# Second FFN, gate and up: seven block products in place of eight for the first four k tiles

## The chip, the cores and the metric

One core of a Trainium2 chip runs the whole kernel. The engines are TensorE (PE; its weight loads are listed apart as PEld), VectorE (DVE), ScalarE (ACT), GpSimd (POOL) and SyncE (SP), which issues most of the DMAs. Every engine takes its instructions in the order of its own queue and waits on semaphores for the others. The metric is the device time in microseconds of one execution, a median over runs; the profile is of one execution.

## The reference

One layer of a streaming encoder on 256 rows (two row tiles of 128) and D = 2048 columns, all in f32. What matters here are the two half-FFNs, one ahead of the mixer and one behind it:

```
x = x + 0.5 * swiglu(rms_norm(x, ffn2_norm), ffn2_w_gate, ffn2_w_up, ffn2_w_down)
swiglu(h, w_gate, w_up, w_down) = (silu(h @ w_gate) * (h @ w_up)) @ w_down
```

w_gate and w_up are 2048 x 5632, w_down is 5632 x 2048. Ahead of the second FFN come the mixer (a state space model and an attention) and its output projection, behind it a gate with a per-layer embedding.

## The kernel before

**Precision.** Each f32 operand is split into two fp32r parts: hi is the rounded copy (ScalarE, L168), lo the rest (VectorE, L171). A product is three matmuls: hi by hi, activation lo by weight hi, activation hi by weight lo. The activation is the stationary operand (128 x 128), the weight the moving one (128 x 512).

**Tiles.** K = 2048 is 16 k tiles of 128. The FFN's columns are 11 blocks (f = 0 to 10) of 512. A raw weight load brings four k tiles of one block, 1 MB, into one of three `raw` buffers (L282). It is split in two halves of two k tiles each; a half's hi and lo (`whi`, `wlo`, four buffers each) are called a weight tile here. `gemm_half` runs one weight tile: two k tiles by two row tiles by three matmuls, 12 in all, the eight that read hi first and the four that read lo last (L292, L293, L297). `gemm_block` does this for the 16 k tiles of one matrix: eight weight tiles.

**The FFN.** For each column block `ffn` runs gate, then up, 16 weight tiles in all. ScalarE turns the gate's sum into silu (L440), VectorE multiplies it with up's sum out of PSUM (L464). Two weight tiles later VectorE transposes the result in 32-blocks into `mid` (L203, `turn_blocks`), and for every pair of blocks 16 DMAs a further eight weight tiles later write the turned activation for the down product (L216). Block 0 of the second FFN instead runs gate and up in turns (`gemm_pair`), because the last quarters of its input come late.

**Order.** `step()` is called after each weight tile and advances whatever was put off. A scheduler then orders the instructions of each engine ahead of time, so what stands in a queue is fixed in the built program. PSUM has four one-bank tiles (`acc`) and two two-bank tiles (`aux`). `sg`, the gate's tile, has one buffer, `h` two. Normalised input: the gain is in the activation parts, the row factor r (`xn.rs`) is applied at the end, to both sums.

Lines of the kernel before that the steps touch: the split 168 and 171, the raw load 282, the matmuls 292, 293 and 297, the silu 440, the final product 464, the transposes 203 and the turning DMAs 216. These lines lie ahead of the change and keep their numbers in the changed kernel, but for 440 and 464, which become 555 and 580 and serve block 0 alone in the second FFN.

Of the kernel before, what the change touches and what calls it, by code (L numbers as in the profile page):

```python
# [9 lines left out]
F32 = mybir.dt.float32  # L10
F32R = mybir.dt.float32r
I32 = mybir.dt.int32
AF = mybir.ActivationFunctionType
ALU = mybir.AluOpType
AX = mybir.AxisListType

P = 128
# [9 lines left out]
NB = 512  # L27
# [6 lines left out]
def layer_kernel(ctx: ExitStack, tc: tile.TileContext, a: dict, shapes: dict, out: bass.AP):  # L34
    nc = tc.nc
# [8 lines left out]
    TT = T // P  # L44
    ND = D // NB
    KD = D // P
# [7 lines left out]
    wp = ctx.enter_context(tc.tile_pool(name="wts", bufs=4))  # L54
# [9 lines left out]
    def uid(s):  # L64
        count[0] += 1
        return f"{s}_{count[0]}"

    def get(pool, tag, width=1024, bufs=1):
        return pool.tile([P, width], F32, tag=tag, name=uid(tag), bufs=bufs)

    def com(tag):
        return get(comp, tag, *{"sg": (1024, 1), "h": (1024, 2), "sq": (NB, 1), "mid": (2048, 1)}[tag])

    def phase(name):
        return tc.tile_pool(name=name, bufs=1, reuse_waits="tile")

    def aux(s="aux"):
        return auxp.tile([P, 1024], F32, tag="aux", name=uid(s))

    def acc(s="acc"):  # L80
        return accp.tile([P, NB], F32, tag="acc", name=uid(s))
# [4 lines left out]
    def halves(kind):  # L86

        return [
            actp.tile([P, 4, T], F32R, tag=kind + s, name=uid(kind + s), bufs={"n": 4, "h": 2}[kind])
            for s in ("hi", "lo")  # L90
        ]
# [4 lines left out]
    def start(g):  # L96
        beside.append(g)
        return g

    def step():  # L100
        for g in list(beside):
            if next(g, beside) is beside:
                beside.remove(g)

    def finish(g):
        for _ in g:
            pass

    def put_off(steps, fn, *args):


        def g():
            for _ in range(steps):
                yield
            fn(*args)

        return start(g())

    def pin(ins):
        return tc.keep_in_program_order(ins)  # L120
# [44 lines left out]
    def split(hi, lo, src, scale=None, pinned=False):  # L165

        if scale is None:
            copy = nc.scalar.copy(hi, src)  # L168
            if pinned:
                pin(copy)  # L170
            nc.vector.tensor_tensor(out=lo, in0=src, in1=hi.bitcast(F32), op=ALU.subtract)  # L171
        else:
            split_each(hi.unsqueeze(1), lo.unsqueeze(1), src.unsqueeze(1), [scale])
# [50 lines left out]
    def by_tile(out, nk):  # L224

        return out.rearrange("p (x f b) -> p f x b", f=nk, b=32)
# [51 lines left out]
    def weight_halves(w, k0, nk, n0, own=None):  # L278

        raw = wp.tile([P, 4, NB], F32, tag="raw", name=uid("raw"), bufs=3)  # L280
        src = w[k0 * P : (k0 + nk) * P, n0 : n0 + NB].rearrange("(j p) n -> p j n", p=P)
        nc.sync.dma_start(raw[:, :nk, :], src)  # L282
        return weight_split(raw, nk, own)

    def gemm_half(ps, half, ts, start, stop, cols=slice(0, NB)):

        (ahi, alo), (h, hi, lo) = half
        for j in range(2):
            for t in ts:
                lh = ahi[:, 2 * h + j, t * P : (t + 1) * P]  # L290
                ll = alo[:, 2 * h + j, t * P : (t + 1) * P]
                nc.tensor.matmul(ps[t], lhsT=lh, rhs=hi[:, j, cols], start=start and j == 0, stop=False)  # L292
                nc.tensor.matmul(ps[t], lhsT=ll, rhs=hi[:, j, cols], start=False, stop=False)  # L293
        for j in range(2):
            for t in ts:
                lh = ahi[:, 2 * h + j, t * P : (t + 1) * P]
                nc.tensor.matmul(ps[t], lhsT=lh, rhs=lo[:, j, cols], start=False, stop=stop and j == 1)  # L297
# [46 lines left out]
    class Normed:  # L344
# [61 lines left out]
        def rs(self, t):  # L406
            return self.r[:, t : t + 1]

    def ffn(i, xn, nxt, bg=None):
        wg, wu, wd = (a[f"ffn{i}_w_{s}"][0] for s in ("gate", "up", "down"))  # L410
        hT = []
        pools = ExitStack()
        early = 8 if bg else NF
        hp = pools.enter_context(phase(f"h{i}"))
        side = ExitStack()
        prep = bg(side) if bg else None
        mids = {}

        def turned(hp, f, hh):
            pair, n_pair = f // 2, min(2, NF - f // 2 * 2) * 4  # L420
            if f % 2 == 0:
                mids[pair] = com("mid")[:, : 128 * TT * n_pair].rearrange(
                    "p (q t f b) -> p q t f b", q=4, t=TT, b=32
                )
            for t in range(TT):
                turn_blocks(mids[pair], hh[:, t * NB : (t + 1) * NB], t, f % 2 * 4, 4)
            if f % 2 or f == NF - 1:
                hf = get(hp, f"hT{pair}", T * n_pair)
                turn_quarters(hf, mids[pair], 8)
                hT.append(by_tile(hf, n_pair))  # L430

        for f in range(NF):
            if prep and f == min(early, NF - 1):
                finish(prep)
                side.close()
                prep = None
                hp = pools.enter_context(phase(f"h{i}b"))
            def gate():
                for t in range(TT):
                    nc.scalar.activation(sg[:, t * NB : (t + 1) * NB], pg[t], AF.Silu, scale=xn.rs(t))  # L440

            first = ()
            if f == 0 and bg:
                warm_up(10)
                first = first_quarters(wg, xn)
            if f == 0 and not bg:
                both = gemm_pair(xn, ((wg, 0), (wu, 0)), KD)
                pg = next(both)
            else:
                pg = gemm_block(xn, wg, f * NB, KD, first)  # L450
            sg = com("sg")
            if f == 0 and bg:
                for n in range(ND):
                    put_off(n, load_x, n)
                    put_off(n + 2, xn.squares, n)
                put_off(6, gate)
            else:
                gate()
            pu = gemm_block(xn, wu, f * NB, KD) if f or bg else next(both)
            if prep and f == 0:  # L460
                start(prep)
            hh = com("h")
            for t in range(TT):
                nc.vector.scalar_tensor_tensor(  # L464
                    out=hh[:, t * NB : (t + 1) * NB], in0=pu[t], scalar=xn.rs(t),
                    in1=sg[:, t * NB : (t + 1) * NB], op0=ALU.mult, op1=ALU.mult,
                )
            put_off(2, turned, hp, f, hh)

        def act(k):  # L470
            hi, lo = halves("h")
            split(in_32(hi), in_32(lo), hT[k // 2][:, k % 2 * 4 : k % 2 * 4 + 4])
            return hi, lo

        for n in range(ND):
            ps = gemm_block(act, wd, n * NB, F // P)
            for t in range(TT):
                nc.vector.scalar_tensor_tensor(
                    out=xt[t][n], in0=ps[t], scalar=0.5, in1=xt[t][n], op0=ALU.mult, op1=ALU.add
                )  # L480
            put_off(0 if n == ND - 1 and n < nxt.early else 2, nxt.block, n)
        pools.close()
# [701 lines left out]
    q0, k0, v0 = SW, SW + NH * DH, SW + 2 * NH * DH  # L1184
    mix, s5p, atp = ExitStack(), ExitStack(), ExitStack()
    mixp = mix.enter_context(phase("mix"))
    pool = s5p.enter_context(phase("s5"))
# [10 lines left out]
    pool = atp.enter_context(phase("attn"))  # L1198
# [19 lines left out]
    both = gemm_pair(lambda k: yss[k], [(sides[0], n * NB) for n in range(2)], SW // P)  # L1218
    for n, side in ((0, 0), (1, 0), (0, 1), (1, 1), (2, 0), (2, 1), (3, 0), (3, 1)):
        y, r = ((yss, rss), (ysb, rsb))[side]  # L1220
        ps = next(both) if n < 2 and not side else gemm_block(lambda k: y[k], sides[side], n * NB, SW // P)
        for t in range(TT):
            nc.vector.scalar_tensor_tensor(
                out=xt[t][n], in0=ps[t], scalar=r[0][:, t : t + 1], in1=xt[t][n], op0=ALU.mult, op1=ALU.add
# [47 lines left out]
    wg = a["w_ple_gate"][0]  # L1272
# [4 lines left out]
    n = ND - 1  # L1277
# [4 lines left out]
    def add(t, n_, r):  # L1282
        x, g = xt[t][n_], es[n_][:, t * NB : (t + 1) * NB]
        nc.vector.scalar_tensor_tensor(out=x, in0=g, scalar=r, in1=x, op0=ALU.mult, op1=ALU.add)
        nc.sync.dma_start(out[0, t * P : (t + 1) * P, n_ * NB : (n_ + 1) * NB], x)

    t = 0
    sigmoid(gate, t, next(gates))
    ple(n, t, gate, next(projs))
    s = small(1)  # L1290
# [7 lines left out]
    t = 1  # L1298
# [3 lines left out]
    early, part, ms, root, r, tmp = (small(1) for _ in range(6))  # L1302
# [9 lines left out]
    for c, (ahead, total) in enumerate(((early, part), (part, ms))):  # L1312
# [3 lines left out]
            out=com("sq")[:, :W], in0=gate[:, cols[c]], scalar=1.0, in1=gate[:, cols[c]], op0=ALU.mult, op1=ALU.mult,  # L1316
# [9 lines left out]
    both = aux()  # L1326
    pin(nc.tensor.matmul(both[:, :NB], lhsT=ident, rhs=xt[t][by_pe], start=True, stop=False, skip_group_check=True))
    for _ in range(10):
# [4 lines left out]
    both = both[:, :NB]  # L1333
# [7 lines left out]
        both, lhsT=diag, rhs=es[by_pe][:, t * NB : (t + 1) * NB], start=False, stop=True, skip_group_check=True  # L1341
# [93 lines left out]
```

## Time and profile before

| what | us |
|---|---|
| median of three runs | 1879.47 (1879.34 to 1879.84) |
| span of the profiled execution | 1878.1 |
| TensorE busy | 1869.5 |
| VectorE busy | 1184.8 |
| ScalarE busy | 963.8 |

The page gives the span of the profiled execution, from the first to the last instruction; it has no separate total time, so the span stands in for it, 1.4 us under the median of the runs. In the views, "x" is a count, "mean ns" the duration of one instruction, and what stands in brackets is the idle time ahead of it on its engine, with what ended it. "us to landing" of a DMA counts from its issue. Matmul durations overlap, since they are pipelined; their spacing is the cost. VectorE's and ScalarE's durations overlap by a little too.

### The profile page before, as it was taken

To read this page: it belongs to the slowest core of one execution; us is meant where nothing else is said; L and a number is where in the kernel's file an instruction comes from. 1 tells how busy PE (TensorE), PEld (TensorE's weight loads), DVE (VectorE), ACT (ScalarE), POOL (GpSimd) and SP (SyncE) were. 2 spreads that over 40 slices of the span, in tenths; PEclk is the share of its full clock that TensorE was granted. 3 is DMA by queue.
4 is the path that set the end of the run, shared out by engine and by line. 5 is a ranking of instruction groups with operands and counts; after the bars stand their busy time and mean duration, and the time that the engine had idled before them with its cause. 6 is when DMAs were issued, how large, how long until landed. Compare 5 with 4: busy or idle time off the path is not lost.

```text
span 1878.1 us, 23877 instructions
## 1 busy us (share of the span) xinstructions
PE 1869.5 (100%) x9194; PEld 1549.5 (83%) x9194; DVE 1184.8 (63%) x1391; ACT 963.8 (51%) x1110; POOL 50.3 (3%) x84
## 2 busy tenths in 40 slices
PE   9999999999999999999999999999999999999998
PEld 7888888888888888888888888888888888888887
DVE  8867665444676776696566655455545566777655
ACT  7444444444455665455785544444444455666554
POOL 0011000000000000010020000000000000000000
PEclk9999999999999999999999999999999999999999
DMA  8788867766665667675646657666667665666563
GB/s 320 246 274 269 265 209 228 225 211 212 207 204 201 197 212 234 186 263 155 217 136 223 222 186 220 195 209 201 205 201 220 191 222 195 203 211 205 181 235 124
DMA packets 230387, 400.07 MB, mean 213 GB/s; under 512 B 26401, under 2 KB 50337, under 8 KB 229985
## 3 DMA queue, kind: packets, MB, share of 16 engines
q1 hardware_dynamic: 227824, 392.81, 65.2%
q0 software_dynamic: 1728, 4.33, 0.7%
q8 instruction: 72, 1.18, 0.3%
q10 hardware_dynamic: 720, 1.41, 0.2%
q14 instruction: 43, 0.34, 0.1%
HBM read 369.26 MB, written 9.83 MB: 202 GB/s over the span
## 4 chain that ended last, share of the span: by engine, by line
PE 97%; ACT 2%; DMA 0%; POOL 0%; issue 0%; SPq 0%; POOLq 0%
PE acc L292 32%; PE acc L297 32%; PE acc L293 32%; PE aux L899 0%; ACT whi L168 0%; DMA raw<-in_ffn_w_gate 0%; ACT nhi L178 0%; POOL sqg L1090 0%; PE aux L843 0%; PE aux L982 0%; PE aux L716 0%; ACT sg L1161 0%; PE aux L1015 0%; ACT L1161 0%; ACT L1034 0%
## 5 line engine op out<-in xcount | busy, mean ns | idle before, releaser
L171 DVE TENSOR_TENSOR wlo<-raw,whi 128x1024 fp32r<-128x1024 f32 x666 | 811.8, 1225 | 587.0 <-ACT whi L168 579.1
L168 ACT CAST whi<-raw 128x1024 fp32r<-128x1024 f32 x666 | 699.5, 1055 | 835.0 <-PE acc L293 776.2
L292 PE MATMUL acc<-whi,nhi 128*128 128x512 f32 x1568 | 613.5, 391 | 0.8 <-ACT whi L168 0.4
L293 PE MATMUL acc<-whi,nlo 128*128 128x512 f32 x1568 | 610.5, 389 | 0.0
L297 PE MATMUL acc<-wlo,nhi 128*128 128x512 f32 x1568 | 420.7, 389 | 0.0
L292 PE MATMUL acc<-whi,hhi 128*128 128x512 f32 x1056 | 410.8, 389 | 0.0
L293 PE MATMUL acc<-whi,hlo 128*128 128x512 f32 x1056 | 410.8, 389 | 0.0
L292 PEld LDWEIGHTS acc<-whi,nhi 128*128 128x128 f32 x1568 | 294.5, 188 | 63.9 <-ACT whi L260 1.3
L297 PEld LDWEIGHTS acc<-wlo,nhi 128*128 128x128 f32 x1568 | 294.3, 188 | 61.7 <-DVE wlo L171 0.4
L293 PEld LDWEIGHTS acc<-whi,nlo 128*128 128x128 f32 x1568 | 294.6, 188 | 60.3
L297 PE MATMUL acc<-wlo,hhi 128*128 128x512 f32 x1056 | 282.2, 389 | 0.0
L293 PEld LDWEIGHTS acc<-whi,hlo 128*128 128x128 f32 x1056 | 198.3, 188 | 41.2
L297 PEld LDWEIGHTS acc<-wlo,hhi 128*128 128x128 f32 x1056 | 198.2, 188 | 41.1
L292 PEld LDWEIGHTS acc<-whi,hhi 128*128 128x128 f32 x1056 | 198.2, 188 | 41.1
L171 DVE TENSOR_TENSOR hlo<-hT,hhi 128x1024 fp32r<-128x1024 f32 x88 | 107.2, 1219 | 0.0
L168 ACT CAST hhi<-hT 128x1024 fp32r<-128x1024 f32 x88 | 91.6, 1042 | 0.1
L464 DVE SCALAR_TENSOR_TENSOR h<-acc,sm,sg 128x512 f32<-128x512 f32 x44 | 31.0, 747 | 23.7 <-PE acc L297 23.7
L440 ACT ACTIVATE sg<-acc,sm 128x512 f32<-128x512 f32 x44 | 27.7, 681 | 6.8 <-PE acc L297 5.1
L203 DVE STREAM_TRANSPOSE mid<-h 128x512 f32<-128x512 f32 x44 | 28.6, 689 | 0.0
L829 POOL COPY dec<-rho 128x512 f32<-128x512 f32 x8 | 9.6, 1233 | 540.9 <-DVE hlo L171 441.6
L1322 POOL TENSOR_SCALAR sm<-sm,sm 128x1 f32<-128x1 f32 x1 | 0.3, 258 | 881.1 <-DVE sq L1315 881.1
L180 DVE SCALAR_TENSOR_TENSOR nlo<-h,gains,nhi 128x256 fp32r<-128x256 f32 x52 | 22.8, 489 | 1.2 <-ACT nhi L178 1.2
(251 smaller groups left out, 657.5 us busy)
## 6 DMA issues: line engine op xcount, KB each, us to landing
raw<-in_ffn_w_up SPq DMA_DIRECT2D x88, 1024.0 KB, 5.7
raw<-in_ffn_w_down SPq DMA_DIRECT2D x88, 1024.0 KB, 5.1
raw<-in_ffn_w_gate SPq DMA_DIRECT2D x86, 1024.0 KB, 5.2
raw<-in_w_in SPq DMA_DIRECT2D x32, 1024.0 KB, 5.7
raw<-in_w_out SPq DMA_DIRECT2D x16, 1024.0 KB, 5.3
raw<-in_w_ple_gate SPq DMA_DIRECT2D x16, 1024.0 KB, 5.4
hT<-mid SPq DMA_DIRECT2D x160, 64.0 KB, 4.9
h<-mid SPq DMA_DIRECT2D x176, 32.0 KB, 3.7
```

The source lines that it names most:

```text
L168: copy = nc.scalar.copy(hi, src)
L171: nc.vector.tensor_tensor(out=lo, in0=src, in1=hi.bitcast(F32), op=ALU.subtract)
L180: nc.vector.scalar_tensor_tensor(out=lo[:, j], in0=src[:, j], scalar=scale, in1=hi[:, j].bitcast(F32), op0=ALU.mult, op1=ALU.subtract,)
L203: nc.vector.transpose(mid[:, :, t, k0 : k0 + nk, :].rearrange("p q f b -> p f q b"), src.rearrange("p (f q b) -> p f q b", f=nk, q=4),)
L292: nc.tensor.matmul(ps[t], lhsT=lh, rhs=hi[:, j, cols], start=start and j == 0, stop=False)
L293: nc.tensor.matmul(ps[t], lhsT=ll, rhs=hi[:, j, cols], start=False, stop=False)
L297: nc.tensor.matmul(ps[t], lhsT=lh, rhs=lo[:, j, cols], start=False, stop=stop and j == 1)
L440: nc.scalar.activation(sg[:, t * NB : (t + 1) * NB], pg[t], AF.Silu, scale=xn.rs(t))
L464: nc.vector.scalar_tensor_tensor(out=hh[:, t * NB : (t + 1) * NB], in0=pu[t], scalar=xn.rs(t), in1=sg[:, t * NB : (t + 1) * NB], op0=ALU.m ...
L829: nc.gpsimd.tensor_copy(dvw[:, e], rho4[:, r0 : r0 + 4].unsqueeze(1).unsqueeze(3).to_broadcast([P, 2, 4, NC]))
L1322: pin(nc.gpsimd.tensor_scalar(total, square, 1.0 / D, ahead, op0=ALU.mult, op1=ALU.add))
```

## The change

In blocks 1 to 10 of the second FFN the first four k tiles of gate and up are computed together. Take the activation's four k tiles as a 2 x 2 block matrix A (rows: row tiles 0 and 1; columns: k tiles 0 and 1, and 2 and 3), and the weights as B (rows: k tiles 0 and 1, and 2 and 3; columns: gate and up; b11 and b21 are gate's halves, b12 and b22 up's). The four output blocks are a product of two 2 x 2 block matrices, which takes eight block products of two k tiles each; here it takes seven, with summed rows of A and summed columns of B:

- weight sums on VectorE (L459): t1 = b11 + b12, t2 = t1 + b22, t4 = t2 + b21, t3 = b12 + b22, two buffers; each is split into hi and lo like a weight (`shi`, `slo`, three buffers). Signs are put into the row sums.
- row sums once, in block 0 (`sum_forms`, L412 to L426), split into hi and lo.
- products in the order b11, b21, t1, t2, t4, t3, b22 (`product`, L452, L453, L455), six matmuls each, with both raw tiles held until all sums are made.
- the products of b21 and t4 stay open in PSUM and take the gate's other 12 k tiles, that of b22 and the bank beside it take up's. After the first four steps the row tiles are done one after the other in each weight tile.
- what the sums share is added at the end: L531 copies the first product out of PSUM (ScalarE), L532 and L533 add the products of t2 and t3 to it, L537 adds the gate's two sums and L538 is the silu, L540 subtracts from the product of t1 (both row tiles at once), L545 adds up's sums, L547 is the final product.

```diff
@@ -406,11 +406,99 @@
         def rs(self, t):
             return self.r[:, t : t + 1]
 
+    def sum_forms(parts):
+
+        hi, lo = parts
+        whole, sums = com("h"), com("h")
+        u = whole.rearrange("p (j t m) -> p j t m", j=4, t=TT)
+        nc.vector.tensor_tensor(
+            out=whole.rearrange("p (j t) -> p j t", j=4), in0=hi.bitcast(F32), in1=lo.bitcast(F32), op=ALU.add
+        )
+        s = sums.rearrange("p (z j m) -> p z j m", z=4, j=2)
+        up, down = u[:, :2], u[:, 2:]
+        for z, (x, y, op) in enumerate((
+            (up[:, :, 1], down[:, :, 1], ALU.subtract), (s[:, 0], up[:, :, 0], ALU.subtract),
+            (up[:, :, 0], up[:, :, 1], ALU.subtract), (down[:, :, 0], s[:, 1], ALU.add),
+        )):
+            nc.vector.tensor_tensor(out=s[:, z], in0=x, in1=y, op=op)
+        both = halves("n")
+        split(*both, sums.rearrange("p (z t) -> p z t", z=4))
+        return both
+
+    def gemm_seven(act, sums, ws, n0, nkt, pool, first, second):
+
+        raws = []
+        for w in ws:
+            raw = wp.tile([P, 4, NB], F32, tag="raw", name=uid("raw"), bufs=3)
+            nc.sync.dma_start(raw, w[: 4 * P, n0 : n0 + NB].rearrange("(j p) n -> p j n", p=P))
+            raws.append(raw)
+        b11, b21, b12, b22 = (raw[:, 2 * h : 2 * h + 2, :] for raw in raws for h in range(2))
+        parts = act(0)
+
+        def whole(k, t):
+            return [[u[:, 2 * k + j, t * P : (t + 1) * P] for j in range(2)] for u in parts]
+
+        def summed(z):
+            return [[u[:, z, j * P : (j + 1) * P] for j in range(2)] for u in sums]
+
+        def product(ps, left, src, own, stop):
+            hi, lo = (
+                (pool if own else wp).tile([P, 2, NB], F32R, tag=s, name=uid(s), bufs=3 if own else None)
+                for s in (("shi", "slo") if own else ("whi", "wlo"))
+            )
+            split(hi, lo, src)
+            lh, ll = left
+            for j in range(2):
+                nc.tensor.matmul(ps, lhsT=lh[j], rhs=hi[:, j], start=j == 0, stop=False)
+                nc.tensor.matmul(ps, lhsT=ll[j], rhs=hi[:, j], start=False, stop=False)
+            for j in range(2):
+                nc.tensor.matmul(ps, lhsT=lh[j], rhs=lo[:, j], start=False, stop=stop and j == 1)
+
+        def add(x, y):
+            t = pool.tile([P, 2, NB], F32, tag="sum", name=uid("sum"), bufs=2)
+            nc.vector.tensor_tensor(out=t, in0=x, in1=y, op=ALU.add)
+            return t
+
+        p1, p2 = acc(), acc()
+        product(p1, whole(0, 0), b11, False, True)
+        product(p2, whole(1, 0), b21, False, False)
+        step()
+        t1 = add(b11, b12)
+        p5 = acc()
+        product(p5, summed(0), t1, True, True)
+        t2 = add(t1, b22)
+        p67 = aux()
+        product(p67[:, :NB], summed(1), t2, True, True)
+        step()
+        t4 = add(t2, b21)
+        p4 = acc()
+        product(p4, whole(1, 1), t4, True, False)
+        t3 = add(b12, b22)
+        product(p67[:, NB:], summed(2), t3, True, True)
+        step()
+        p38 = aux()
+        product(p38[:, :NB], summed(3), b22, False, False)
+        step()
+        put_off(0, first, p1, p67)
+        for w, banks, fresh in ((ws[0], [p2, p4], False), (ws[1], [p38[:, :NB], p38[:, NB:]], True)):
+            for k0 in range(4, nkt, 4):
+                part = act(k0 // 4)
+                for half in list(weight_halves(w, k0, 4, n0)):
+                    begin = k0 == 4 and half[0] == 0
+                    end = k0 + 4 >= nkt and half[0] == 1
+                    for t in range(TT):
+                        gemm_half({t: banks[t]}, (part, half), (t,), fresh and t == 1 and begin, end)
+                    step()
+            if not fresh:
+                put_off(0, second, p2, p4, p5)
+        return p38
+
     def ffn(i, xn, nxt, bg=None):
         wg, wu, wd = (a[f"ffn{i}_w_{s}"][0] for s in ("gate", "up", "down"))
         hT = []
         pools = ExitStack()
         early = 8 if bg else NF
+        sevens = None if bg else pools.enter_context(phase(f"sums{i}"))
         hp = pools.enter_context(phase(f"h{i}"))
         side = ExitStack()
         prep = bg(side) if bg else None
@@ -435,6 +523,33 @@
                 side.close()
                 prep = None
                 hp = pools.enter_context(phase(f"h{i}b"))
+            if sevens and f:
+                sg, hh = com("sg"), com("h")
+                gate_cols, up_cols = ([u[:, t * NB : (t + 1) * NB] for t in range(TT)] for u in (sg, hh))
+
+                def opened(p1, p67, g=gate_cols, u=up_cols):
+                    nc.scalar.copy(g[0], p1)
+                    nc.vector.tensor_tensor(out=u[0], in0=p67[:, :NB], in1=g[0], op=ALU.add)
+                    nc.vector.tensor_tensor(out=u[1], in0=p67[:, NB:], in1=u[0], op=ALU.add)
+
+                def gated(p2, p4, p5, g=gate_cols, u=up_cols, hh=hh):
+                    for z, (ps, other) in enumerate(((p2, g[0]), (p4, u[1]))):
+                        nc.vector.tensor_tensor(out=g[z], in0=ps, in1=other, op=ALU.add)
+                        nc.scalar.activation(g[z], g[z], AF.Silu, scale=xn.rs(z))
+                    v = hh.rearrange("p (t n) -> p t n", t=TT)
+                    nc.vector.tensor_tensor(
+                        out=v, in0=p5.unsqueeze(1).to_broadcast([P, TT, NB]), in1=v, op=ALU.subtract
+                    )
+
+                p38 = gemm_seven(xn, sums, (wg, wu), f * NB, KD, sevens, opened, gated)
+                nc.vector.tensor_tensor(out=hh, in0=p38, in1=hh, op=ALU.add)
+                for t in range(TT):
+                    nc.vector.scalar_tensor_tensor(
+                        out=up_cols[t], in0=up_cols[t], scalar=xn.rs(t), in1=gate_cols[t], op0=ALU.mult, op1=ALU.mult
+                    )
+                put_off(2, turned, hp, f, hh)
+                continue
+
             def gate():
                 for t in range(TT):
                     nc.scalar.activation(sg[:, t * NB : (t + 1) * NB], pg[t], AF.Silu, scale=xn.rs(t))
@@ -446,6 +561,7 @@
             if f == 0 and not bg:
                 both = gemm_pair(xn, ((wg, 0), (wu, 0)), KD)
                 pg = next(both)
+                sums = sum_forms(xn(0))
             else:
                 pg = gemm_block(xn, wg, f * NB, KD, first)
             sg = com("sg")
```

## The prediction

> **What bounds the kernel now.** I read the first part of the page, the clock, the shares of the chain that ended last, and then one column block of the second FFN's gate and up in the stage view and in order of time.
>
> ```profile
> span 1878.1 us, 23877 instructions
> PE 1869.5 (100%) x9194; PEld 1549.5 (83%) x9194; DVE 1184.8 (63%) x1391; ACT 963.8 (51%) x1110; POOL 50.3 (3%) x84
> ...
> PEclk9999999999999999999999999999999999999999
> ...
> PE 97%; ACT 2%; DMA 0%; POOL 0%; issue 0%; SPq 0%; POOLq 0%
> ```
>
> TensorE runs all the time at the full clock and is the chain. A matmul taken away is therefore time taken away, and a wait put in front of a matmul is time added. The next fence is the stage view of one whole block (columns: TensorE, its loads, VectorE, ScalarE, GpSimd, clock, DMA share, GB/s), then the end of one block and the start of the next in order of time.
>
> ```profile
> 1182.68:1226.20 43.52, 43.52 (x193) 36.04 (x192) 22.02 (x21) 18.07 (x19) 0.00 (x0) 1.00 0.61 194
> ```
>
> ```profile
> 1179.96 0.39 PE L292 MATMUL acc<-whi,nhi 128*128 128x512 f32 x1
> ...
> 1180.35 1.23 DVE L171 TENSOR_TENSOR wlo<-raw,whi 128x1024 fp32r<-128x1024 f32 x1 [1.50 <-ACT whi L168]
> ...
> 1181.98 1.06 ACT L168 CAST whi<-raw 128x1024 fp32r<-128x1024 f32 x1 [1.66 <-PE acc L293]
> 1182.66 1.41 DVE L464 SCALAR_TENSOR_TENSOR h<-acc,sm,sg 128x512 f32<-128x512 f32 x2 [1.09 <-PE acc L297]
> 1182.68 0.39 PE L292 MATMUL acc<-whi,hhi 128*128 128x512 f32 x1
> ...
> 1183.98 1.22 DVE L171 TENSOR_TENSOR wlo<-raw,whi 128x1024 fp32r<-128x1024 f32 x1
> ...
> 1185.12 1.30 DVE L203 STREAM_TRANSPOSE mid<-h 128x512 f32<-128x512 f32 x2
> 1185.23 0.37 SPq L282 DMA_DIRECT2D raw<-in_ffn_w_up  x1
> 1185.40 0.39 PE L292 MATMUL acc<-whi,hhi 128*128 128x512 f32 x1
> ```
>
> A weight tile (two k tiles, 12 matmuls) takes 1182.68 to 1185.40, 2.72 us, or 0.2267 us a matmul; 192 of them are the 43.52 us. ScalarE's cast starts 2.02 us into a tile, when the hi matmuls have let go of a buffer: it fills the tile four ahead. So TensorE has three tiles, 8 us, in hand, and VectorE idles 1.5 us per tile. Back to back VectorE's spacing is less than the duration: two L464 take 1.32 us (1182.66 to 1183.98), a split 1.14 (to 1185.12). The raw load is issued 0.03 us after the split that frees its buffer (1185.20).
>
> **The change, part by part.**
>
> *Matmuls.* In ten of eleven blocks the first four k tiles took 48 matmuls and take 42. 60 x 0.2267 = 13.6 us less, if nothing waits. Six matmuls in a row now go to one bank; the last block of the final gate (per-layer embedding) already does that, and its pace is the same:
>
> ```profile
> 1846.82 0.39 PE L292 MATMUL acc<-whi,nhi 128*128 128x512 f32 x1
> ...
> 1848.19 0.39 PE L292 MATMUL acc<-whi,nhi 128*128 128x512 f32 x1
> ```
>
> Six in 1.37 us. So this edit costs nothing of itself.
>
> *VectorE and ScalarE on average.* The prices (groups with shapes: of the block ending at 1182.68, then of the whole span):
>
> ```profile
> L171 DVE TENSOR_TENSOR wlo<-raw,whi 128x1024 fp32r<-128x1024 f32 x16 | 19.6, 1222 | 20.4 <-ACT whi L168 18.9 <-DMA hT<-mid 1.5
> L168 ACT CAST whi<-raw 128x1024 fp32r<-128x1024 f32 x17 | 18.0, 1057 | 27.1 <-PE acc L293 27.1
> L203 DVE STREAM_TRANSPOSE mid<-h 128x512 f32<-128x512 f32 x2 | 1.3, 690 | 0.0
> L440 ACT ACTIVATE sg<-acc,sm 128x512 f32<-128x512 f32 x2 | 1.3, 680 | 0.0
> ```
>
> ```profile
> L725 DVE TENSOR_TENSOR t<-bt,coef 128x1024 f32<-128x1024 f32 x8 | 9.7, 1221 | 0.1
> L860 DVE TENSOR_TENSOR rt<-aux,rot 128x1024 f32<-128x1024 f32 x4 | 4.9, 1222 | 6.1 <-PE aux L843 6.1
> L1284 DVE SCALAR_TENSOR_TENSOR x<-e,sm,x 128x512 f32<-128x512 f32 x7 | 4.8, 748 | 0.1
> L1252 DVE TENSOR_TENSOR h<-acc,h 128x512 f32<-128x512 f32 x7 | 4.5, 684 | 7.3 <-PE acc L297 7.3
> ```
>
> Seven splits for four: +3 x 1.222. Four weight sums (priced as L725): 4 x 1.221. Four 512-wide adds from PSUM (L532, L533, two L537; as L1252): 4 x 0.684. L540 and L545 (as L860): 2 x 1.222. The two final products stay at 0.748. Together 13.7 us, so VectorE goes from 22.0 to 35.7 us in a block of 42.2; ScalarE from 18.1 by three casts and a copy to 21.9. Neither becomes the bound on average. But nearly all of it falls around the 9.5 us of the seven products, where a buffer feeds 6 matmuls (1.36 us) instead of 12 (2.72), and that stretch must be walked.
>
> *The order.* Both engines run in the built program's order, which has two forms. Form A (blocks 1, 2, 4, 6, 8, 10; block 1 with the old finish), VectorE: sums t1, t2; splits b11, t1, b21, t2; sum t4; split b22; L545 of the block before; split t4; its two L547; sum t3; its two transposes; split of the next gate tile, R1; split t3. Form B (3, 5, 7, 9): splits b11, b21; t1, t2; splits t1, b22; L545; split t2; two L547; t4; a transpose; t3; split t4; a transpose; split t3.
>
> *When it can start.* Let the first product start at 0, so the twelfth tile R12 starts at -2.72 and R7 at -16.32. t1 needs both raw tiles; up's is loaded into the buffer that the split of R10 frees. That split stands behind the two L537, and the second of these waits for R6's last matmul: -16.1 to -15.4. The split ends at -14.2, the load is issued and lands 5.6 us later (limits 5.0 and 6.4), at -8.6:
>
> ```profile
> raw<-in_ffn_w_up SPq DMA_DIRECT2D x40, 1024.0 KB, 5.6
> raw<-in_ffn_w_gate SPq DMA_DIRECT2D x37, 1024.0 KB, 5.2
> ```
>
> ```profile
> DMA to landing us min/median/max: 5.0/5.6/6.4
> ```
>
> VectorE is then free (R12's split, whose cast waits for R8's hi matmuls, ends at -8.8).
>
> *Form A.* From -8.6: t1 1.25 (t2 needs its result, so its full duration), eleven more of 1024 columns at the spacing 1.14, two L547 1.32, two transposes 1.22 (0.61 each: the 1.30 for two less the last one's 0.69). That is 16.3 us: the split of t3 starts at 7.7 and ends at 9.0. TensorE reaches that product, the sixth, at 5 x 1.36 = 6.8. Its hi part is cast at 7.1 (on ScalarE it stands behind the cast of R3, whose load follows t4 and lands 5.2 us on), and its lo part is wanted at 8.0. Wait 0.3 + 1.0 = 1.3 us.
>
> *Form B.* The split of b21 comes first, and its cast waits for R10's hi matmuls (-5.7): cast to -4.6, split to -3.4. Only then t1 (1.25), t2 (1.3, since the next split waits for t1's cast) and four spacings of 1.14, which bring L547 to 3.7; t4 ends at 6.3, its cast at 7.35; t3 ends at 8.0, split t4 at 9.2, split t3 at 10.9. TensorE wants t4's hi at 5.44 (1.9 late), its lo 0.9 later than it then comes to it, t3's lo 0.4 later. Wait 3.2 us.
>
> Block 1 has no L545 ahead of the chain: 0.2. Sum of the waits: 0.2 + 5 x 1.3 + 4 x 3.2 = 19.5 us. What is late next recovers: R2's split is 3 us early in either form, and each later tile gives back 1.5.
>
> *Other edits.* The forms of the summed rows (L414 to L427) add four 256-wide adds and two 1024-wide instructions to VectorE, about 4 us, in block 0, whose VectorE idles half the time:
>
> ```profile
> 1080.00:1090.00 10.00, 10.00 (x46) 8.28 (x45) 4.61 (x4) 3.67 (x4) 0.00 (x0) 1.00 0.58 185
> ```
>
> Zero; without the cover at most those 4 us. DMA: the same loads and bytes. L433 on SP's queue holds back nothing needed sooner: in form B the second gate load follows t4 and lands at 11.5, and R3 is due at 18. L537 on VectorE holds R10's split, counted above. The other PSUM readers wait for groups already closed.
>
> *Sum.* -13.6 + 19.5 = +5.9 us. On the profiled span 1878.1 that is 1884.0; the runs' median 1879.47 lies 1.4 above the span, so 1885.4, taken as 1885.5. The ends of the waits: load landing in 5.0 us gives form A 1.0 and 17.9 in all (1883.8); every spacing at the row's full 1.22 instead of 1.14 gives 2.2 and 3.8, 26.4 in all (1892.3), and a landing at 6.4 besides some 0.8 more per form A (1896). I take 1.14, because it is measured between just such neighbours. A shorter spacing than 1.14 is not in the rows, but the sums are no splits: at 1.05 the waits would be 12.9, level with the saving.
>
> [...]
>
> **Rivals.** *Faster (the waits stay under the saving).* One mechanism: the queue from the up load's landing to the split of t3 is shorter than walked, since TensorE's three tiles in hand, or tighter spacing of the sums, cover it. It decides at a mean wait of 1.36 us per block, a queue about 0.7 us shorter in both forms. For it: VectorE's 1.5 us idle per tile; against: the lead is one of buffers that hold half as much work here. With no wait at all, 1879.5 - 13.6 = 1865.9. *No change.* The same queue 0.2 to 1 us shorter: 1876 to 1883. *Longer.* Full durations and late landings together: 1896 and above. *The clock.* If TensorE's waits, up to 1.9 us each, made it run the next tile at half speed, each block would lose another 2.7 us: 1912. Every row here has 1.00, but none has such waits. [...] That the change removes fewer matmuls than said is excluded: the built order has the six per block gone.
>
> **How the numbers follow.** What a measurement can tell from no change is 0.2%, 3.8 us. The forecast, slower by 4 to 17 us, has 0.66; longer 0.05 and the clock 0.02; no change 0.17; faster 0.10. The range 1880 to 1897 takes in the ends above and the upper part of no change. Slower 0.73, same 0.17, faster 0.10.
>
> **What would show it.** Right: 60 matmuls fewer; TensorE idle in every block at L452 or L455, on VectorE's split or ScalarE's cast of a sum, about 1.3 us in even blocks and 3 us in odd ones from 3 on; blocks of 43.5 and 45.4 us in turn (42.16 plus the wait). Wrong: blocks of 42.2 us with no idle (the lead covers), waits at the first or second product (loads late), or at R1 to R4 (VectorE not recovering), or a granted clock under 1.

## The result and the profile after

The changed kernel takes 1871.32 us (median of four runs, 1870.86 to 1872.24) where the kernel before, measured beside it, takes 1879.65 us. The ratio is 0.9954, with a 95% interval of 0.9940 to 0.9968: it is faster by 8.3 us; the ratio gives 0.46%. The forecast was 1885.5 us with a range of 1880 to 1897, and slower as the likeliest case. It was wrong in sign.

The page of the changed kernel, its first part, its clock row and the shares of the chain that ended last:

```profile
span 1870.4 us, 23938 instructions
...
PE 1859.4 (99%) x9134; PEld 1536.3 (82%) x9134; DVE 1310.4 (70%) x1527; ACT 996.5 (53%) x1151; POOL 50.4 (3%) x84
...
PEclk9999999999999999999999999999999999999999
...
PE 92%; ACT 3%; DVE 2%; DMA 1%; SPq 1%; issue 1%; POOL 0%; DVEq 0%; ACTq 0%; POOLq 0%
```

The 60 matmuls are gone (9194 to 9134), VectorE has 125.6 us more work, and TensorE is still busy 99% of the span. The stage view of two blocks in a row (columns: length, then busy time and count of TensorE, its loads, VectorE, ScalarE and GpSimd, then clock, DMA share and GB/s):

```profile
1139.79:1182.26 42.47, 42.47 (x187) 34.83 (x186) 31.14 (x31) 20.55 (x22) 0.00 (x0) 1.00 0.71 223
1182.26:1225.14 42.88, 42.74 (x187) 34.68 (x186) 37.31 (x37) 22.09 (x24) 0.00 (x0) 1.00 0.57 196
```

A block of 186 matmuls without a wait would be 186 x 0.2267 = 42.17 us; before it was 43.52. So block 2 loses 0.3 us to waits and block 3 0.7, where 1.3 and 3.2 were forecast. The even blocks that follow lose 0.2 each and the odd ones 0.7 to 0.8. Over the ten blocks the waits come to 4.1 us (block 1 has 0.1), not 19.5. The groups of TensorE's waits in the ten blocks (its loads' rows, in total, times, longest) show the same:

```profile
PEld aux L452 <- ACT shi L168: 2.7, 5, 0.6
PEld aux L455 <- DVE slo L171: 1.0, 4, 0.2
PEld acc L452 <- ACT shi L168: 0.9, 4, 0.2
PEld acc L297 <- DVE wlo L171: 0.9, 4, 0.2
```

A load's row counts time in which the matmuls before it still run (at 1191.36, in block 3, the row has 0.57 us, and the matmul before ends at 1191.22, 0.14 us ahead), so the rows don't add up to the 4.1 us. The first three stand where the waits were forecast, at the products of the sums, on the cast or split of a sum; the fourth, 0.2 us a time, is an ordinary weight tile. Only the size is a fifth. What makes them short is seen in the order of time. First block 2 (form A), from its first matmul; TensorE and VectorE only:

```profile
1139.79 0.39 PE L452 MATMUL acc<-whi,hhi 128*128 128x512 f32 x1
...
1146.73 0.50 PE L452 MATMUL aux<-shi,nhi 128*128 128x512 f32 x1
...
1147.20 1.21 DVE L171 TENSOR_TENSOR slo<-sum,shi 128x1024 fp32r<-128x1024 f32 x1
...
1147.76 0.40 PE L452 MATMUL aux<-whi,nhi 128*128 128x512 f32 x1
...
1148.70 0.62 PE L455 MATMUL aux<-slo,nhi 128*128 128x512 f32 x2
...
1149.16 0.63 PE L455 MATMUL aux<-wlo,nhi 128*128 128x512 f32 x2
```

VectorE makes t3's lo from 7.41 to 8.62 us into the block, much as walked (7.7 to 9.0). But TensorE does not ask for it at 8.0. The matmuls of the seventh product, b22's (`aux<-whi`, L452), stand in its queue between t3's hi and t3's lo. The lo is wanted at 8.91 us, and it is there. Then block 3 (form B):

```profile
1187.75 0.40 PE L452 MATMUL aux<-whi,nhi 128*128 128x512 f32 x1
...
1188.68 0.62 PE L455 MATMUL aux<-wlo,nhi 128*128 128x512 f32 x2
...
1189.14 0.40 PE L292 MATMUL acc<-whi,hhi 128*128 128x512 f32 x1
...
1189.60 0.46 PE L452 MATMUL acc<-shi,hhi 128*128 128x512 f32 x1
...
1190.07 1.22 DVE L171 TENSOR_TENSOR slo<-sum,shi 128x1024 fp32r<-128x1024 f32 x1
...
1190.59 0.40 PE L292 MATMUL acc<-whi,hhi 128*128 128x512 f32 x1
...
1191.36 0.50 PE L452 MATMUL aux<-shi,nhi 128*128 128x512 f32 x1
...
1191.70 0.63 PE L455 MATMUL acc<-slo,hhi 128*128 128x512 f32 x2
1191.83 1.19 DVE L171 TENSOR_TENSOR slo<-sum,shi 128x1024 fp32r<-128x1024 f32 x1
...
1193.54 0.63 PE L455 MATMUL aux<-slo,nhi 128*128 128x512 f32 x2
```

Here the whole product of b22 (1187.75 to 1189.14) and two matmuls of the next gate tile R1 (L292, line 292 being the ordinary weight tiles) run before t4's product starts at 1189.60, and more of R1's matmuls stand between t4's hi and lo and between t3's hi and lo. t4's hi is taken at 7.34 us into the block instead of 5.44, t3's lo at 11.28, when VectorE has had it ready since 10.76 (walked 10.9).

The sum against the spans: -13.6 + 4.1 = -9.5, measured 1870.4 - 1878.1 = -7.7. The other 1.8 us lie ahead of the change: block 1 starts 1.9 us later than before. Most of that is one row of the waits ahead of it:

```profile
PE aux L959 <- issue: 1.4, 1, 1.4
```

L959 is a matmul of the state-space stage that the change does not touch; whether this belongs to the change is tested below.

### The profile page after: what moved, and what is told of

It is laid out like the page before. It is cut to its first block, busy times and chain, and to the rows that moved or that the text cites. A ratio compares the mean times of both kernels' runs of the same rounds, so it can differ in the third digit from the quotient of the medians.

```text
span 1870.4 us, 23938 instructions
## 1 busy us (share of the span) xinstructions
PE 1859.4 (99%) x9134; PEld 1536.3 (82%) x9134; DVE 1310.4 (70%) x1527; ACT 996.5 (53%) x1151; POOL 50.4 (3%) x84
## 4 chain that ended last, share of the span: by engine, by line
PE 92%; ACT 3%; DVE 2%; DMA 1%; SPq 1%; issue 1%; POOL 0%; DVEq 0%; ACTq 0%; POOLq 0%
PE acc L292 26%; PE acc L297 26%; PE acc L293 26%; PE aux L293 3%; PE aux L292 3%; PE aux L297 3%; ACT whi L168 1%; SPq L1061 1%; PE acc L455 1%; DMA raw<-in_w_in 1%; PE aux L452 1%; PE acc L452 1%; PE acc L453 1%; PE aux L455 1%; PE aux L453 1%
## 5 line engine op out<-in xcount | busy, mean ns | idle before, releaser
L171 DVE TENSOR_TENSOR wlo<-raw,whi 128x1024 fp32r<-128x1024 f32 x656 | 798.2, 1224 | 458.9 <-ACT whi L168 455.3
L292 PE MATMUL acc<-whi,nhi 128*128 128x512 f32 x1408 | 551.0, 391 | 1.2 <-ACT whi L260 0.5
L293 PE MATMUL acc<-whi,nlo 128*128 128x512 f32 x1408 | 548.2, 389 | 0.0
L292 PE MATMUL acc<-whi,hhi 128*128 128x512 f32 x816 | 317.6, 389 | 0.0
L293 PE MATMUL acc<-whi,hlo 128*128 128x512 f32 x816 | 317.5, 389 | 0.0
L292 PEld LDWEIGHTS acc<-whi,nhi 128*128 128x128 f32 x1408 | 264.3, 188 | 58.3 <-ACT whi L168 1.7
L297 PE MATMUL acc<-wlo,hhi 128*128 128x512 f32 x816 | 221.0, 389 | 0.0
L297 PEld LDWEIGHTS acc<-wlo,hhi 128*128 128x128 f32 x816 | 152.8, 188 | 32.5 <-DVE wlo L171 0.9
L292 PEld LDWEIGHTS acc<-whi,hhi 128*128 128x128 f32 x816 | 153.1, 188 | 31.8
L171 DVE TENSOR_TENSOR hlo<-hT,hhi 128x1024 fp32r<-128x1024 f32 x88 | 107.1, 1218 | 0.0
L292 PE MATMUL aux<-whi,nhi 128*128 128x512 f32 x160 | 62.2, 389 | 0.0
L293 PE MATMUL aux<-whi,nlo 128*128 128x512 f32 x160 | 62.2, 389 | 0.0
L297 PE MATMUL aux<-wlo,nhi 128*128 128x512 f32 x160 | 49.3, 389 | 0.0
L171 DVE TENSOR_TENSOR slo<-sum,shi 128x1024 fp32r<-128x1024 f32 x40 | 48.6, 1214 | 0.4 <-ACT shi L168 0.2
```

## The experiments

Theory 1: VectorE's and ScalarE's queues are as walked, and what hides the waits is the order of TensorE's queue, which the build fills with ready matmuls ahead of each late split. Rivals: the queues of VectorE are shorter than walked; the gain is something that happens once (the row sums, block 1), not per block.

**All products in written order on TensorE.** The matmuls of the seven products, and the matmuls that read hi in the tiles of the same blocks behind them, are kept in the order in which the program writes them (`pin` tells the scheduler to keep an instruction in that order).

```diff
-                nc.tensor.matmul(ps, lhsT=lh[j], rhs=hi[:, j], start=j == 0, stop=False)
+                pin(nc.tensor.matmul(ps, lhsT=lh[j], rhs=hi[:, j], start=j == 0, stop=False))
...
-                        gemm_half({t: banks[t]}, (part, half), (t,), fresh and t == 1 and begin, end)
+                        gemm_half({t: banks[t]}, (part, half), (t,), fresh and t == 1 and begin, end, keep=pin)
```

> The changed kernel, with TensorE held to the order in which the seven products and the tiles behind them are written (b11, b21, t1, t2, t4, t3, b22, then the next gate tile) in all ten blocks; VectorE's queue stays nearly as it was. Theory 1 (the walk of VectorE's queue was right, but the built program lets TensorE do the product of b22 and matmuls of the next tile while it would wait for t4 and t3): the waits come back, about 1.3 us in the even blocks and 3.2 in the odd ones from 3 on, 19.5 us in place of the 4.1 measured, so about 15 us slower than the changed kernel, 1886. Rival (the walk was wrong, three tiles in hand cover the queue): 1871, as the changed kernel, within 2 us.

Measured: 1886.44 us (1884.88 to 1888.44), ratio 1.0029 [1.0017, 1.0040]. That is 6.1 us over the kernel before measured beside it (1880.30); the forecast was 6.0 over its 1879.47. Against the changed kernel it is some 14 us slower (7.7 to 8.3 us under the kernel before in its two measurements), with the same number of instructions on each engine. Stage view of blocks 2, 5 and 3 and the groups of TensorE's waits in the ten blocks:

```profile
1138.36:1181.64 43.28, 42.82 (x187) 34.76 (x186) 31.20 (x31) 20.70 (x22) 0.00 (x0) 1.00 0.72 219
1271.42:1316.70 45.28, 43.13 (x188) 34.69 (x186) 37.16 (x37) 22.30 (x24) 0.00 (x0) 1.00 0.57 186
1181.64:1228.15 46.51, 44.41 (x187) 35.91 (x186) 37.25 (x37) 22.30 (x24) 0.00 (x0) 0.96 0.55 181
```

```profile
PE acc L452 <- ACT shi L168: 6.0, 4, 1.5
PE aux L455 <- DVE slo L171: 3.1, 5, 0.7
PE acc L455 <- DVE slo L171: 2.3, 4, 0.6
```

The even blocks wait 43.28 - 42.17 = 1.1 us (walked 1.3), block 5 3.1 (walked 3.2), with t4's hi as the longest wait, 1.5 us in each of the four blocks of form B. VectorE is where it was, but for two splits ahead of these that change places in form B. Its splits of t4 and t3 in block 3:

```profile
1189.31 1.22 DVE L171 TENSOR_TENSOR slo<-sum,shi 128x1024 fp32r<-128x1024 f32 x1
...
1191.07 1.19 DVE L171 TENSOR_TENSOR slo<-sum,shi 128x1024 fp32r<-128x1024 f32 x1
```

They start 7.67 and 9.43 us into the block, in the changed kernel 7.81 and 9.57; in block 2 t3's split starts at 7.41 in both. So what changed is TensorE's order. Theory 1 stands; shorter queues on VectorE are excluded, since they would have hidden the waits in this order too. Block 3 shows something more: its clock is 0.96 in the mean. In finer windows:

```profile
1188.00:1190.00 2.00, 1.19 (x4) 0.67 (x4) 2.00 (x3) 1.24 (x2) 0.00 (x0) 1.00 0.49 96
1190.00:1192.00 2.00, 1.42 (x4) 1.18 (x5) 2.00 (x3) 0.55 (x1) 0.00 (x0) 0.72 1.04 400
1192.00:1194.00 2.00, 2.00 (x6) 1.52 (x6) 2.00 (x3) 1.01 (x1) 0.00 (x0) 0.50 0.99 331
1194.00:1196.00 2.00, 2.00 (x10) 1.61 (x9) 2.00 (x3) 0.80 (x2) 0.00 (x0) 0.92 0.76 237
```

After waits of 1.5 and 0.6 us the granted clock falls to 0.50 for about 3 us, and the block is 46.51 - 45.28 = 1.2 us longer. Block 9 does the same (46.31); blocks 5 and 7, with the same waits, keep the full clock. So part of the agreement with the forecast is luck: without the clock the waits of the ten blocks come to some 18 us, not 19.5, and in the profiled execution the half clock adds 2.3.

**Seven products in five blocks only** (f = 6 to 10), and **the row sums alone** (no block uses them).

```diff
-            if sevens and f:
+            if sevens and f > 5:
```

```diff
-            if sevens and f:
+            if sevens and f > NF:
```

> Seven products in blocks 6 to 10 only. If each block gains the same (1.36 less 0.41 of waits, measured over ten blocks), half of the gain: 1879.65 - 4.8 = 1874.9. If something is lost once, ahead of the ten blocks (the trace of the changed kernel is 1.9 us later than before at the start of block 1), 1876.7.

> The summed rows are made in block 0 and then not used; all blocks take the old way. If their 4 us on VectorE are covered and nothing is lost once: 1879.6. If the 1.9 us by which block 1 of the changed kernel starts late come from the summed rows or go with any change of the program: 1881.5. If the summed rows are not covered: up to 1883.6.

Measured: 1875.18 us with five blocks (ratio 0.9973 [0.9962, 0.9984], 5.1 us under the kernel before in the same comparison, 1880.3); 1880.17 us with the row sums alone (ratio 0.9998 [0.9989, 1.0007]). The gain is one of each block, about 1 us, and the row sums in block 0 are free. The interval with five blocks, 1873.2 to 1877.3 us, is too wide to tell a loss of 1.8 us once from none; its trace does, for that execution: block 6 starts at 1313.43 (before 1313.24), and the span is 1873.0, 5.1 less than before.

**b22's product written third,** so that it is ahead of the late sums by the program itself.

```diff
+        p38 = aux()
+        product(p38[:, :NB], summed(3), b22, False, False)
         t1 = add(b11, b12)
...
-        p38 = aux()
-        product(p38[:, :NB], summed(3), b22, False, False)
         put_off(0, first, p1, p67)
```

> The product of b22, which needs no sum, is written third in place of seventh; the sums follow later. Theory 1 (what is left of the waits is TensorE reaching the products of t4 and t3 ahead of VectorE's splits): most of the 4.1 us of waits go, 1868 to 1870. Rival (the waits are a matter of VectorE's load, whatever the order): 1871, no change. A loss, if the third product has to wait for L545 to empty its bank: over 1872.

Measured: 1872.91 us (ratio 0.9955 [0.9942, 0.9969]), no gain over the changed kernel: a miss. Its odd blocks take 43.17 to 43.21 us against 42.88, its even ones 42.36 to 42.39, as in the changed kernel. What this was to bring, the built order had brought already. The waits that its trace shows are on casts and splits of sums, none on L545. Its profiled execution is the slowest of its five, and block 1 starts 4.5 us later than before. The wait for nothing at L959, here 2.2 us long, is half of that. Most of the rest is the clock: after one wait of 1.8 us at L1190, a matmul in the mixer, it fell to half; in the two windows below that is 2 x 0.35 + 2 x 0.50 = 1.7 us.

```profile
976.00:978.00 2.00, 2.00 (x8) 1.57 (x7) 1.69 (x6) 1.26 (x2) 0.00 (x0) 0.65 0.95 339
978.00:980.00 2.00, 2.00 (x6) 1.63 (x5) 0.62 (x4) 1.05 (x1) 0.00 (x0) 0.50 1.00 324
```

Seven other profiles, the one of the kernel before included, have that wait of 1.7 to 1.8 us. In four of them the mean clock is 1.000 (here 0.999), and in the three others block 1 starts 0.3 to 0.4 us later than before, which leaves no room for these 1.7 us.

**The changed kernel again,** beside the next three.

> The changed kernel once more, beside the kernels below. Theory 1 (the built order of TensorE's queue hides nearly all waits, about 4 us of waits stay in the ten blocks): 1871.3 us, blocks of 42.4 (even) and 42.9 us (odd) as in the first look. The 1.4 us in which TensorE waited for nothing the profile shows, in the state-space stage far ahead of the change: if it belongs to single executions and not to the change, it is gone or of another size here, and the span is up to 1.4 us below 1870.4; if the change puts it there, it is 1.4 us again.

Measured: 1872.66 us, ratio 0.9955 [0.9942, 0.9967]. In this execution there is no such row at L959, block 1 starts at 1095.78 (before 1095.64), and the span is 1869.7. The sum closes: -13.6, +5.1 of waits (block 1 has 0.9 here, 0.1 in the first profile), +0.1 ahead of the blocks, together -8.4 us, and the spans differ by 1869.7 - 1878.1 = -8.4. The 1.4 us at L959 came in one execution of this program and not in the other. Whether the kernel before has it in some of its own, its one profile can't show.

**The products in written order, the gate tile free.** As the first experiment, but only the seven products are kept in order; matmuls of the gate tile may move between them. The edit against the first experiment:

```diff
-                        gemm_half({t: banks[t]}, (part, half), (t,), fresh and t == 1 and begin, end, keep=pin)
+                        gemm_half({t: banks[t]}, (part, half), (t,), fresh and t == 1 and begin, end)
```

> The seven products stay in written order on TensorE, but the matmuls of the gate tile behind them may move between them; in the blocks with the second order of VectorE the build puts four of these ahead of t4's product (0.91 us of work), and in the others four ahead of t3's low half. Theory 1 (any matmul that is ready and stands ahead of the late split takes its own length off the wait): the even blocks' wait of 1.1 falls to 0.2 as in the changed kernel, the odd blocks' 3.1 falls to 1.4 (t4's high half 1.5 - 0.9, its low half 0.6, t3's low half 0.7 - 0.45), against 0.7 in the changed kernel: 4 x 0.7 = 3 us more than it, about 1874. Rival (only the move of b22's product ahead of t4's carries the gain): odd blocks near 45.2 as with everything in written order, about 1881 us.

Measured: 1877.77 us (ratio 0.9983 [0.9974, 0.9992]), 5.1 over the changed kernel beside it, where theory 1 has 3 and the rival 10. The span is 1875.1, 5.4 over the changed kernel's second profile. Stage view of blocks 2 and 3, and the waits of TensorE:

```profile
1139.04:1181.66 42.62, 42.53 (x187) 34.86 (x186) 31.20 (x31) 20.65 (x22) 0.00 (x0) 1.00 0.71 222
1181.66:1225.84 44.18, 42.88 (x188) 34.78 (x186) 37.31 (x37) 22.27 (x24) 0.00 (x0) 1.00 0.57 190
```

```profile
PE acc L452 <- ACT shi L168: 2.8, 4, 0.7
PE acc L455 <- DVE slo L171: 2.4, 4, 0.6
```

Four matmuls of the gate tile, 0.91 us, ahead of t4's product take its wait from 1.5 to 0.7 us; t4's lo, which nothing new stands ahead of, waits 0.6 as it did. In the even blocks four gate matmuls do what b22's did: from the fourth block on they take 42.35 to 42.39 us. So ready matmuls of another tile will do as well, theory 1. The size was off: the odd blocks lose 2.0 us, not 1.4. The two rows give 1.3 of it; here a wait cost more than its row says. In the first experiment's block 3, in order of time:

```profile
1186.67 0.62 PE L455 MATMUL aux<-slo,nhi 128*128 128x512 f32 x2
...
1188.79 0.50 PE L452 MATMUL acc<-shi,hhi 128*128 128x512 f32 x1 [1.50 <-ACT shi L168]
1189.13 0.39 PE L453 MATMUL acc<-shi,hlo 128*128 128x512 f32 x1
```

The next start was due at 1186.67 + 2 x 0.227 = 1187.12 and came 1.67 us later. The row counts only 1.50, because it counts from the end of the matmul before (1186.67 + 0.62 = 1187.29), and matmul durations overlap. The one after it came at 0.34 instead of 0.23: together 1.78 us for a wait listed as 1.50. Two such waits bring the 1.3 to about 1.9. Of the 2.4 us by which the built order shortens an odd block (45.28 to 42.88), 1.1 is thus had by the gate tile's matmuls alone and the other 1.3 comes with b22's product moved ahead of t4's.

**VectorE in form A in all blocks,** TensorE left to the build, and then **the same with TensorE in written order.** The second sum, the splits behind t1 and the finish of the block before are kept in the order of form A.

```diff
+        t1 = add(b11, b12, False)
+        t2 = add(t1, b22)
+        h11 = halved(b11, False)
+        h1 = halved(t1, True)
+        h21 = halved(b21, False)
+        h2 = halved(t2, True)
+        t4 = add(t2, b21)
+        h22 = halved(b22, False)
...
-                nc.vector.tensor_tensor(out=hh, in0=p38, in1=hh, op=ALU.add)
+                put_off(0, closed, p38)
```

> VectorE takes the first order (t1, t2, then the splits; the up columns of the block before behind them) in all ten blocks; TensorE's order is left to the build. Theory 1 (the odd blocks' extra 0.5 us is the late t4 and t3 of the second order): odd blocks fall from 42.9 to 42.4, 4 x 0.5 = 2 us, about 1869.3. Rival (the second order costs nothing by itself since TensorE's queue was filled for it, and a new order on TensorE loses as much): 1871 to 1873.

> VectorE as in the run before, and TensorE's matmuls in written order in all blocks. Theory 1 (the two queues together set the wait: 1.1 us in each block of the first order, as measured with TensorE in written order): all blocks at 43.3, ten times 1.1 = 11 us against the 4 us of the changed kernel, about 1878. Rival (VectorE's order doesn't matter once TensorE goes by the written order): 1886 as measured with that alone. The waits stay at 1.1 in one piece, so that the granted clock stays at 1.0 here, where it fell to 0.5 in two blocks with 3.1 us of waits.

Measured: 1874.49 us (ratio 0.9966 [0.9954, 0.9979]) and 1891.42 us (ratio 1.0051 [1.0037, 1.0064]). The first is 1.8 us over the changed kernel, 1.5 past its rival's upper end: odd blocks take 43.42 us instead of 42.88. The second misses both times that were expected, and the clock did not stay at 1.0. Its even blocks take 43.29 us, as form A should, but its odd ones 45.46 to 48.30. The reason is in VectorE's queue, block 2 first, then block 3 (starting at 1139.99 and 1183.28; L465 is the sum, L171 `slo` the splits of t1, t2 and t4):

```profile
1131.13 1.22 DVE L465 TENSOR_TENSOR sum<-raw,raw 128x1024 f32<-128x1024 f32 x1
...
1141.47 1.22 DVE L171 TENSOR_TENSOR slo<-sum,shi 128x1024 fp32r<-128x1024 f32 x1
...
1175.69 1.23 DVE L465 TENSOR_TENSOR sum<-raw,raw 128x1024 f32<-128x1024 f32 x1 [1.18 <-DMA raw<-in_ffn_w_up]
...
1179.63 1.23 DVE L171 TENSOR_TENSOR slo<-sum,shi 128x1024 fp32r<-128x1024 f32 x1 [0.31 <-ACT shi L168]
...
1182.39 1.23 DVE L171 TENSOR_TENSOR slo<-sum,shi 128x1024 fp32r<-128x1024 f32 x1 [0.40 <-ACT shi L168]
...
1186.94 1.22 DVE L171 TENSOR_TENSOR slo<-sum,shi 128x1024 fp32r<-128x1024 f32 x1
```

In the odd block VectorE waits for the up load, so t1 starts 7.59 us ahead of the block and not 8.86, and it waits twice more for casts, 0.31 and 0.40. Together that is 2.0 us, and t4's split is 2.2 us later (3.66 into the block instead of 1.48). Form B, which puts the splits of b11 and b21 ahead of t1, starts t1 at -3.46 (1178.80 in the changed kernel), long after the load, and has no use for an early landing. So form B is no loss that one order would cure. Why the up load lands later ahead of odd blocks (6.6 us after its issue, at most 5.4 ahead of block 2) was not tested. The rest is the clock: stage view of block 3, two windows.

```profile
1193.00:1195.00 2.00, 1.16 (x4) 0.78 (x3) 2.00 (x2) 0.00 (x0) 0.00 (x0) 0.60 1.02 396
1195.00:1197.00 2.00, 2.00 (x6) 1.54 (x6) 1.82 (x3) 0.00 (x0) 0.00 (x0) 0.50 0.41 96
```

Block 9 keeps the full clock and takes 45.46; block 3, at half clock for some 6 us, takes 48.30, 2.8 us more. Blocks 5 and 7 lie between (46.97 and 46.27), with the clock at 0.50 for a shorter time.

No version here beats the changed kernel. Of its 4 to 5 us of waits some could still be had; earlier up loads would need a fourth raw buffer or one for up's first load alone, which was not tried.

## Why the prediction was wrong

- *Matmuls, -13.6 us:* right. 60 are gone, and the blocks nearly without waits take 42.3 to 42.4 us (42.17 worked out), and six in a row to one bank keep the pace (the second product of block 2, 1141.15 to 1142.51, 1.36 us).
- *VectorE and ScalarE on average:* right. VectorE 31.1 and 37.3 us in blocks 2 and 3, 34.2 in the mean (35.7 worked out), ScalarE 20.6 and 22.1 (21.9). Neither is the bound.
- *The order on VectorE:* right, two forms in the blocks named. *When it can start:* right, up's load issued at -14.23 (walked -14.2), t1 at -8.85 (-8.6). *The walk:* right, t3's split ends at 8.62 in form A (9.0), t4's and t3's in form B at 9.03 and 10.76 (9.2 and 10.9).
- **The step that failed: "TensorE reaches that product, the sixth, at 5 x 1.36 = 6.8", "its lo part is wanted at 8.0", and in form B "TensorE wants t4's hi at 5.44".** The prediction goes by the built order of VectorE and ScalarE in every form of block, but for TensorE it takes the written order in all ten blocks. Only block 1 of the changed kernel runs in that order. From block 2 on the build reorders TensorE's queue as well: it puts b22's product, written last, and hi matmuls of the next gate tile ahead of whatever half was late. The lo of t3 is wanted at 8.91 and t4's hi at 7.34. The waits are 4 to 5 us, not 19.5. With that one assumption made true, the first experiment gives 1886.44 against 1885.5 forecast, with waits of 1.1 and 3.1 us against 1.3 and 3.2; that the totals agree within 1 us owes some 2 us to the half clock in two blocks.
- *What is late next recovers, and other edits at zero:* right. The ordinary tiles show no wait over 0.2 us, and the row sums alone measure 0.9998.
- *Rivals:* "faster" came, at a mean wait of 0.4 to 0.5 us where 1.36 decides, but not by its mechanism: the queue from the load to t3's split was not shorter than walked; the user of its result came later. That TensorE's own order could change was on no list, and so the chance of faster, 0.10, was too low.
- *The clock:* no part in the result (1.00 in every block of the changed kernel). The words "none has such waits" overlook one: the profile of the kernel before has a wait of 1.8 us in the mixer (`PE aux L1074 <- POOL sqg L1090: 1.8, 1, 1.8`), with the clock at 1.00. The rival's chance of 0.02 was an estimate of the author's, and where the waits were real the clock did fall, to the half speed that the rival supposes: to 0.50 after waits of 1.5 and 0.6 us within about 3.5 us. It fell with no single wait of a matmul listed longer than 1.8 us, and in the first experiment and the last it came back after 3 to 6 us. The half clock cost 1.2 us in a block of the first experiment and 2.8 in the worst of the last, where 2.7 had been estimated.

## What to carry to other kernels

Where a scheduler orders the queues, a wait has two ends, and both have to be read from the built program in every form that the block takes: when the result is ready, and when its user comes up in its own queue. Here the first was right to within 0.4 us and the second, taken from the written order, turned the sign. A late operand cost 0.2 us in an even block with ready work standing ahead of it on TensorE and 1.1 us without; here matmuls of another tile covered it as well as a product of the same block did (42.35 to 42.39 us a block against 42.35 to 42.37). An order that looks better on the feeding engine can lose when it puts a later load at its head (odd blocks 43.42 us against 42.88).

## What was not expected of the hardware

- The granted clock fell to 0.50 after TensorE had waited only 1.5 and 0.6 us within some 3.5 us, in two of four blocks with the same waits (blocks 3 and 9, not 5 and 7). In one of eight profiles with a wait of 1.7 to 1.8 us in the mixer it fell to 0.50 after that wait alone. What decides was not found.
- A wait listed as 1.50 us took 1.78 us from the work: 0.17 us because the row counts from the end of the matmul before, behind the start that was due, and 0.11 because the second matmul after the wait came that much later than the usual spacing.
- TensorE lost 1.4 us (2.2 in one other execution) at one matmul of the state-space stage with no wait that the profile shows, in one execution of the changed kernel and not in the other, in two of eight profiles. It hid about a sixth of the gain in the first profile, and only a second profile of the same kernel told it from the change.
